# Opening two gate pairs with narrow products ahead of the plain feed-forward tiles

## The chip, the cores and the metric

The program runs on one core of a Trainium2 chip. The core has five engines that the text names as the profile does: PE (matrix products into the accumulation banks; PEld is its weight load), DVE (elementwise operations), ACT (activations and copies), POOL (here small scalars and DMA issues) and SP (DMA issues). Each engine works through its own list of instructions; semaphores make one wait for another. The metric is the device time of one launch in microseconds (us); less is better.

## What is computed

A two-layer decoder trunk on 512 tokens of width 1024 in float32: layer 0 has a gated short convolution, layer 1 windowed attention, and each layer ends in a SwiGLU feed-forward of inner width 2816. The change is in the feed-forward alone, which is run once per layer:

```python
def swiglu(h, w_gate_up, w_down):
    g, u = jnp.split(h @ w_gate_up, 2, axis=-1)
    return (jax.nn.silu(g) * u) @ w_down

for l in range(DEPTH):
    ...
    ff = swiglu(rmsnorm(h, ffn_pre_norm[l]), ffn_w_gate_up[l], ffn_w_down[l])
    h = h + rmsnorm(ff, ffn_post_norm[l])
```

## The kernel before

**Three products for one.** Every float32 factor is split into a high and a low part. `mm3` (L207) issues three matmuls for a product: high weight by low input, high by high, low weight by high input. A weight tile of 128x1024 arrives from memory as `raw`, ACT rounds it to `whi`, and DVE subtracts to get `wlo` (L500, L501).

**Plain tiles.** The inner width has 22 tiles of 128. The first two (`PLAIN = 2`) are plain: gate and up of each, so four products of 128 inner columns by all 512 tokens over eight blocks of the 1024 inputs. `project_first` (L1158) makes the four side by side in four banks (`pgu`). It goes over the first 256 tokens and then over the second 256, since those tokens' normalised input is finished later: after six blocks of the first half come the transposes of the last token tiles (`turn`), their splits (`split`), the copies of input parts (`keep`), and in the second half the seven-product factors (`factors`, L389). `gate_pair` (L1188) then applies Silu on ACT and the product with up on DVE.

**Gate pairs.** The other 20 tiles are ten pairs `q`. For each, gate and up of two tiles (256 columns) by the 512 tokens are a 2x2 block matrix, and `gate_jobs` (L1203) computes it in seven block products instead of eight. Product 1 is the gate's weights for the first half of the inputs by the first half of the tokens; product 2 the gate's weights for the second half of the inputs by the same tokens; 1 and 2 add up to the gate of the first 256 tokens. The other five (6, 5, 7, 3, 4) use sums of weight blocks and of input blocks (`factors`). A product has four blocks of inputs and two tiles `e`. The products run in the order 1, 2, 6, 5, 7, 3, 4. 1, 6, 7 and 4 are accumulated one upon the other in the two banks of chain X (tile `gx`), 5 and 3 in chain Z (`gz`), 2 has chain Y (`gy`). Chain X is *broad*: one matmul of 512 columns takes the high weight by high and low input side by side, and one of 256 the low weight by the high input. The others are narrow (`mm3` on 256 columns).

Because a chain goes on in the same bank, each stage has to be read out before the next product of the chain may write. `take(p)`, called right behind each product, does that: for 1, 6 and 4 ACT copies one half of each bank and DVE adds the other (L1260, L1237), for 7 DVE adds both halves, for 5 ACT copies, for 2 and 3 DVE adds. After 4, two DVE operations (L1264) multiply gate by up. `st`, `u` and `gr` are the tiles that hold these.

**The line of jobs.** `in_line` (L505) sets the order. Each product is a job; after job j it prepares the weights of job j+3 (ACT then DVE), then forms the sum of two raw tiles for the next one where a pair needs it (`add`, L488; pairs in `ADDED`, among them pair 1), then takes one part of the earlier pairs' input sums for the down product from a list (`pair_sums` L601: `a`, `s`, `alo`). Instructions of an engine stand in its list in this order. `manual_schedule` keeps it for PE, DVE, ACT and POOL; SP's DMA issues are placed by the scheduler. Behind pair 2 come the down products of the first round (`down_jobs`), then the next pairs.

**Weights in advance.** `Ahead` (L418) fetches and splits the first weights of a feed-forward while the stage before (`close`) still runs: four plain weights there, then two more that `last_tile` (L1132) splits between its steps; these are the blocks for products 1 and 2 of pair 0. There are 7 raw buffers and 4 pairs of weight buffers (`wsp`); `slots` puts a weight into other tiles instead. The pools of banks are `ps_mm` (4), `ps_sc` (2) and `ps_pt` (2).

Of the kernel before, what the change touches and what calls it, by code (L numbers as in the profile page):

```python
# [16 lines left out]
P = 128  # L17
D = 1024
S = 512
# [4 lines left out]

PLAIN = 2

ADDED = (1, 2, 3, 4, 5, 7)
# [56 lines left out]
def yoco_kernel(  # L84
# [46 lines left out]
    def wide(s, dt=F32):  # L131
        return wides.tile([P, D], dt, tag="wide", name=name(s))
# [124 lines left out]
    class Update:  # L257
# [130 lines left out]

        def factors(self):  # L389

# [7 lines left out]
            for j in range(2):  # L398
# [733 lines left out]
    def last_tile(res, pieces, ahead=None):  # L1132


        def some(i):
            for n, *f in pieces[i]:
                if n == "keep":
                    res.keep(f[0], 0, f[1])
# [18 lines left out]

    def project_first(pss, ws, x, then):  # L1158
        for hf in range(2):
            c = slice(hf * 256, (hf + 1) * 256)  # L1160

            for ks in ((0, 1), *((k,) for k in range(2, KT))):
                for ps, (whi, wlo) in zip(pss, ws):
                    for k in ks:
                        kk = slice(k * P, (k + 1) * P)
                        mm3(ps[:, c], whi[:, kk], wlo[:, kk],
                            x[k][0][:, c], x[k][1][:, c], k == 0, k == KT - 1)
                for k in ks:
                    then(hf, k)
# [12 lines left out]
    def ffn(l, before, ahead, gain, gpres, following):  # L1182
# [5 lines left out]
        def gate_pair(pg, pu):  # L1188
# [12 lines left out]
            return pair_sums(gr, acts[0])  # L1201

        def gate_jobs(q, factors, out, to, then):  # L1203


# [12 lines left out]
            pools = {"X": ps_mm, "Y": ps_pt, "V": ps_pt, "Z": ps_sc}  # L1218
            split = {}
            if q == 0:  # L1220

                pools = {"X": ps_sc, "Y": ps_pt, "V": ps_pt, "Z": ps_mm}
                raws[1], raws[2] = [], []
                split = {1: ahead.ready[4], 2: ahead.ready[5]}
            banks, kept = {}, []

            def tiles(a):
                return a.rearrange("p (e c) -> p e c", e=2)

            def take(p):  # L1230
                x, y, z, v = (banks.get(c) for c in "XYZV")
                st, u, gr = kept
                g0, g1 = (gr.rearrange("p (e h c) -> p e h c", e=2, h=2)[:, :, h]
# [4 lines left out]

                if p == 2:
                    add(g0, tiles(y), tiles(st))  # L1240
# [26 lines left out]
            def run(p):  # L1267
                def products(job):
                    if not kept:
                        kept.extend([slot("st"), slot("st"), wide("gr")])  # L1270
                    whi, wlo = split[p] if p in split else job.w
                    c = chain[p]
# [25 lines left out]
            def end():  # L1298
# [46 lines left out]
        mix = [None] * NB  # L1345
        pss = [bank("pgu", ps_mm) for _ in range(4)]
        with tc.manual_schedule(engines=ALL):
            last_tile(before, [
                [(0, 4)], [(0, 5), ("keep", 0, False), ("weights",)],
                [], [("keep", 1, True), (0, 6), (0, 7), ("keep", 3, True)],  # L1350
                [("keep", 2, False), ("weights",)]], ahead)

            def then(hf, k):
                if hf == 0 and k in (5, 6):
                    for b in ((0, 1), (2, 3))[k - 5]:
                        before.turn(b, (2,))
                if hf == 0 and k == 6:
                    for b in range(4):
                        before.turn(b, (3,))
                    for f in range(KT):  # L1360
                        before.split(0, f, 1)
                    for b in range(4):
                        before.keep(b, 1)
                if hf == 1 and k == 1:
                    factors.update(before.factors())
                if hf == 1 and k == 3:
                    if l == 0:
                        sum_on("o1")
                    sum_on(f"{l}f0")

            factors = {}
            project_first(pss, ahead.ready[:4], xs, then)

            def late():
                parts = [gate_pair(*pss[i : i + 2]) for i in (0, 2)][1]
                sum_on(f"{l}f1")
                return parts

            jobs, behind_one = [], []
            for rd, (f0, f1) in enumerate(ROUNDS):  # L1380
# [565 lines left out]
```

## Time and profile before

| what | value |
|---|---|
| median of 3 runs | 1010.04 us (1009.71 to 1010.2) |
| profiled execution | 1010.16 us |
| its span, first to last instruction | 1008.3 us |
| granted PE clock, mean | 0.998 |
| most frequent group on DVE: low parts of weights (L501) | x231, 279.0 us, mean 1212 ns |
| most frequent group on ACT: high parts of weights (L500) | x231, 239.7 us, mean 1051 ns |
| DMA moved | 246.61 MB, mean 245 GB/s |

The feed-forward of layer 0 begins near 176.7 us in the span, that of layer 1 near 671 us. Rows of the order of time give the start, the duration, the engine, the line, the operation, output and inputs, shapes and a count where equal ones follow each other; a bracket tells idle time ahead and who ended it. Successive instructions of DVE and ACT overlap by a little, so their price in a list is the distance from one start to the next.

### The profile page before, as it was taken

How to read it: one execution, taken by the hardware profiler on the slowest of the kernel's cores; microseconds unless marked ns; L12 is line 12 of the kernel's file. 1: busy time of each engine (PE TensorE's matmuls, PEld its weight loads, DVE VectorE, ACT ScalarE, POOL GpSimd, SP SyncE). 2: the span in 40 equal slices, each digit the busy share in tenths (PEclk: the TensorE clock that was granted, in tenths of full speed). 3: DMA queues.
4: the chain of work that ended last, by engine and by line, in shares of the span. 5: the costliest groups of instructions: out<-in, count | busy, mean ns of one | idle time of the engine just before them, and what ended most of it. 6: DMA issues, size and time to landing. Idle time of an engine off the chain costs nothing. (4 is left out here: it accounts for less than half of the span.)

```text
span 1008.3 us, 16460 instructions
## 1 busy us (share of the span) xinstructions
PE 999.5 (99%) x6008; PEld 887.4 (88%) x6008; DVE 911.2 (90%) x1564; ACT 609.5 (60%) x1105; POOL 184.6 (18%) x250
## 2 busy tenths in 40 slices
PE   9999999999999999999999999999999999999997
PEld 8899888999889898898898888799998988989986
DVE  7898877899799999999888998989997999999996
ACT  7445545875655455566485788777666564646641
POOL 0211021212101011000022756321201010110001
PEclk9999999999999999999999999999999999999999
DMA  9885988669979699779504889966999587978742
GB/s 342 266 253 172 335 291 289 200 198 286 342 236 298 225 301 317 241 217 333 198 1 136 216 241 250 278 259 170 311 281 315 167 253 239 300 259 271 244 169 83
DMA packets 67872, 246.61 MB, mean 245 GB/s; under 512 B 8016, under 2 KB 8784, under 8 KB 56016
## 3 DMA queue, kind: packets, MB, share of 16 engines
q1 hardware_dynamic: 52624, 148.14, 39.5%
q0 software_dynamic: 14592, 96.48, 37.6%
q8 instruction: 47, 0.77, 0.3%
q10 hardware_dynamic: 576, 0.95, 0.3%
q14 instruction: 33, 0.27, 0.1%
HBM read 239.25 MB, written 102.76 MB: 339 GB/s over the span
## 5 line engine op out<-in xcount | busy, mean ns | idle before, releaser
L501 DVE TENSOR_TENSOR wlo<-raw,whi 128x1024 fp32r<-128x1024 f32 (+1 forms) x231 | 279.0, 1212 | 26.5 <-ACT whi L500 26.3
L500 ACT ACTIVATE whi<-raw 128x1024 fp32r<-128x1024 f32 (+1 forms) x231 | 239.7, 1051 | 79.1 <-DVE raw L488 37.6
L1282 PE MATMUL gx<-xt,whi 128*128 128x512 f32 x480 | 120.6, 393 | 0.0
L1282 PEld LDWEIGHTS gx<-xt,whi 128*128 128x128 f32 x480 | 86.2, 189 | 15.7
L571 POOL DMA_DIRECT2D hsum<-in_w_gb_dram x96 | 63.7, 727 | 160.8 <-ACT whi L500 107.5
L571 POOL DMA_DIRECT2D hsum<-hsum x32 | 25.3, 790 | 351.5 <-ACT whi L500 257.7
L1260 ACT ACTIVATE st<-gx 128x256 f32<-128x256 f32 x120 | 43.5, 380 | 60.8 <-PE gx L1285 57.2
L1237 DVE TENSOR_TENSOR st<-gx,st 128x256 f32<-128x256 f32 x200 | 77.4, 417 | 2.2 <-ACT st L1260 0.4
L1285 PEld LDWEIGHTS gx<-xt,wlo 128*128 128x128 f32 x480 | 65.5, 190 | 4.7
L1285 PE MATMUL gx<-xt,wlo 128*128 128x256 f32 x480 | 66.9, 282 | 0.0
L1296 ACT ACTIVATE gr<-gr 128x1024 f32<-128x1024 f32 x20 | 21.2, 1062 | 55.8 <-DVE gr L1237 55.8
L208 PE MATMUL gy<-xlo,whi 128*128 128x256 f32 x176 | 49.8, 283 | 0.0
L209 PE MATMUL gy<-xhi,whi 128*128 128x256 f32 x176 | 49.8, 283 | 0.0
L210 PE MATMUL gy<-xhi,wlo 128*128 128x256 f32 x176 | 49.8, 283 | 0.0
L208 PE MATMUL px<-wlo,ahi 128*128 128x512 f32 x120 | 46.7, 389 | 0.0
L209 PE MATMUL px<-whi,ahi 128*128 128x512 f32 x120 | 46.7, 389 | 0.0
L210 PE MATMUL px<-whi,alo 128*128 128x512 f32 x120 | 46.7, 389 | 0.0
L571 POOL DMA_DIRECT2D hsum<-in_w_dn_dram x48 | 32.1, 765 | 69.0 <-ACT whi L500 47.4
L1282 PE MATMUL gx<-xhl,whi 128*128 128x512 f32 x160 | 39.9, 391 | 0.0
L672 DVE TENSOR_TENSOR mix<-mix,px 128x512 f32<-128x512 f32 x54 | 34.8, 679 | 2.1 <-PE px L210 2.1
L318 POOL TENSOR_TENSOR ur<-uv,mhalf 128x1 f32<-128x1 f32 x15 | 13.9, 928 | 115.0 <-DVE uv L313 114.9
L488 DVE TENSOR_TENSOR raw<-raw,raw 128x1024 f32<-128x1024 f32 x28 | 34.1, 1218 | 0.1
(359 smaller groups left out, 3052.4 us busy)
## 6 DMA issues: line engine op xcount, KB each, us to landing
hsum<-in_w_gb_dram POOLq DMA_DIRECT2D x96, 512.0 KB, 8.0
raw<-hsum SPq DMA_DIRECT2D x88, 512.0 KB, 8.1
raw<-in_w_gb_dram SPq DMA_DIRECT2D x60, 512.0 KB, 7.1
hsum<-in_w_dn_dram POOLq DMA_DIRECT2D x36, 512.0 KB, 8.0
raw<-in_w_dn_dram SPq DMA_DIRECT2D x32, 512.0 KB, 7.0
hsum<-hsum POOLq DMA_DIRECT2D x28, 512.0 KB, 5.6
hsum<-in_w_dn_dram POOLq DMA_DIRECT2D x12, 768.0 KB, 13.0
raw<-in_w_in_dram SPq DMA_DIRECT2D x13, 512.0 KB, 7.2
```

The source lines that it names most:

```text
L208: nc.tensor.matmul(out, whi, xlo, start=start, stop=False, **kw)
L209: nc.tensor.matmul(out, whi, xhi, start=False, stop=False, **kw)
L210: nc.tensor.matmul(out, wlo, xhi, start=False, stop=stop, **kw)
L488: nc.vector.tensor_tensor(out=raw, in0=raw, in1=self.raws[1].tile, op=ALU.add)
L500: self.begun = nc.scalar.activation(hi[:, :n], raw, AF.Copy)
L501: nc.vector.tensor_tensor(out=lo[:, :n], in0=raw, in1=hi[:, :n].bitcast(F32), op=ALU.subtract)
L571: nc.gpsimd.dma_start(dst, src, max_dma_last_dim=4 * 4 * S, **kw))
L672: nc.vector.tensor_tensor(out=m, in0=m, in1=banks[bs][r], op=ALU.subtract if half else ALU.add)
L1237: nc.vector.tensor_tensor(out=out, in0=a, in1=b, op=ALU.add)
L1260: nc.scalar.activation(ste, a, AF.Copy)
L1282: nc.tensor.matmul(banks[c][e], whi[:, kk], factors[p][k][2], start=opened and k == 0, stop=False, **kw)
L1285: nc.tensor.matmul(banks[c][e][:, :256], wlo[:, kk], factors[p][k][0], start=False, stop=k == 3 and p in (4, 5), **kw)
```

## The change

Two gate pairs (`OPENED = 2`) now begin ahead of the plain tiles. For each, products 1 and 2 are made narrow in one bank (`Opening`): product 1 over input blocks 0 to 3, a copy of the bank by ACT (`one`, into `st`), product 2 accumulated on top over blocks 4 to 7, and a copy of the sum by ACT into the gate's place (`two`, into `gr`). The four weights that are ready first are therefore those of these products; the four plain weights come behind. The plain tiles are then made one after the other over all 512 tokens (`project`), as four jobs at the head of the line. Pairs 0 and 1 have five jobs left, 6, 5, 7, 3, 4. Since their X chain begins at 6, product 1 has to be added by DVE: `take` for these pairs uses no ACT any more (four adds for 6 and 4, one for 5). Pair 1's first two blocks are still loaded in the line as well, for the sums that 6 and 3 need.

```diff
-        def factors(self):
+        def factors(self, between):
...
+                if j == 0:
+                    between()
...
     def first_weights(l):
-        return ([w_gu[l, f, j] for f in range(2) for j in range(2)]
-                + [w_gb[l, 0, b] for b in range(2)])
+        return ([w_gb[l, q, b] for b in range(2) for q in range(OPENED)]
+                + [w_gu[l, f, j] for f in range(PLAIN) for j in range(2)])
...
+        class Opening:
+            def __init__(self, q):
+                self.ws = ahead.ready[q], ahead.ready[OPENED + q]
+                self.x = bank("gx", ps_mm)
+                self.st, self.gr = slot("st"), wide("gr")
+
+            def products(self, *ks):
+                for k in ks:
+                    whi, wlo = self.ws[k // 4]
+                    for e in range(2):
+                        kk = slice(e * S + k % 4 * P, e * S + (k % 4 + 1) * P)
+                        mm3(self.x[:, e * 256 : (e + 1) * 256], whi[:, kk], wlo[:, kk],
+                            *(a[:, :256] for a in xs[k]), e == k == 0, e == 1 and k == KT - 1,
+                            skip_group_check=True)
+
+            def one(self):
+                nc.scalar.activation(self.st, self.x, AF.Copy)
+
+            def two(self):
+                out = self.gr.rearrange("p (e h c) -> p e h c", e=2, h=2)[:, :, 0]
+                nc.scalar.activation(out, self.x.rearrange("p (e c) -> p e c", e=2), AF.Copy)
...
+                if early and p == 6:
+                    both = slot("st")
+                    kept.append(both)
+                    for e in range(2):
+                        c = slice(e * 256, (e + 1) * 256)
+                        add(both[:, c], x[e][:, :256], st[:, c])
+                        add(both[:, c], x[e][:, 256:], both[:, c])
+                elif early and p == 5:
+                    add(u, z, st)
+                elif early and p == 3:
+                    add(g1, tiles(z), tiles(kept[3]))
+                elif early and p == 4:
+                    for e in range(2):
+                        c = slice(e * 256, (e + 1) * 256)
+                        add(st[:, c], x[e][:, :256], st[:, c])
+                        add(st[:, c], x[e][:, 256:], st[:, c])
...
-                    for p in (1, 2, 6, 5, 7, 3, 4)]
+                    for p in (1, 2, 6, 5, 7, 3, 4)[2 if early else 0 :]]
...
+            ahead.fetch(2)
+            opened_pairs = first, second = [Opening(q) for q in range(OPENED)]
+            for pair_of in opened_pairs:
+                pair_of.products(*range(4))
             last_tile(before, [
-                [(0, 4)], [(0, 5), ("keep", 0, False), ("weights",)],
-                [], [("keep", 1, True), (0, 6), (0, 7), ("keep", 3, True)],
+                [(0, 4)],
+                [(0, 5), ("keep", 0, False), ("do", first.one)],
+                [("do", second.one)],
+                [("keep", 1, True), (0, 6), (0, 7), ("keep", 3, True)],
                 [("keep", 2, False), ("weights",)]], ahead)
...
+            first.products(4, 5)
+            second.products(4, 5)
+            for b in range(2):
+                before.turn(b, (2,))
+            first.products(6, 7)
...
+            second.products(6, 7)
+            for f in range(KT):
+                before.split(0, f, 1)
+            first.two()
+            ahead.slots()
+            second.two()
+            ahead.hi()
+            for b in range(4):
+                before.keep(b, 1)
+            ahead.lo()
+            ahead.hi()
+            factors = before.factors(ahead.lo)
...
+            def plain_job(n):
+                def run(job):
+                    pss.append(bank("pgu", ps_mm))
+                    project(pss[n], ahead.ready[2 * OPENED + n], xs)
...
-            jobs, behind_one = [], []
+            jobs, behind_one = [plain_job(n) for n in range(2 * PLAIN)], []
```

What this does to the lists of the engines is shown at three places of layer 0. The first is DVE ahead of and at the taking of pair 1's product 6 (`gx` of pair 1 into `st`), which has to be over before PE may write product 7 on the same banks. Before:

```order
L614 TENSOR_TENSOR a_472_2476<-gr_2253,a_472_2476 128x256
L1237 TENSOR_TENSOR gr_2479<-gy_2510,st_2477 128x2x256
L501 TENSOR_TENSOR wlo_2537<-raw_2280,whi_2536 128x1024
L488 TENSOR_TENSOR raw_2233<-raw_2233,raw_2231 128x1024
L617 TENSOR_TENSOR s_2474<-gr_2253 128x256
L618 SCALAR_TENSOR_TENSOR s_2474<-s_2474,gr_2253 128x256
L1237 TENSOR_TENSOR st_2477<-gx_2480,st_2477 128x256
L1237 TENSOR_TENSOR st_2477<-gx_2481,st_2477 128x256
```

And now, where `gx_2288` and `gx_2289` are pair 0's banks and `gx_2450`, `gx_2451` pair 1's:

```order
L1250 TENSOR_TENSOR gr_1887<-gz_2320,st_2306 128x2x256
L505 TENSOR_TENSOR wlo_2407<-raw_2149,whi_2406 128x1024
L628 TENSOR_TENSOR alo_2411<-s_2284,ahi_2410 128x512
L1250 TENSOR_TENSOR st_1886<-gx_2288,st_1886 128x256 x2
L1250 TENSOR_TENSOR st_1886<-gx_2289,st_1886 128x256 x2
L1293 SCALAR_TENSOR_TENSOR gr_1887<-st_1886,gr_1887 128x2x256
L1293 SCALAR_TENSOR_TENSOR gr_1887<-st_2287,gr_1887 128x2x256
L505 TENSOR_TENSOR wlo_2438<-raw_2211,whi_2437 128x1024
L492 TENSOR_TENSOR raw_2247<-raw_2247,raw_2147 128x1024
L628 TENSOR_TENSOR alo_2443<-s_2285,ahi_2442 128x512
L1250 TENSOR_TENSOR st_2468<-gx_2450,st_1889 128x256
L1250 TENSOR_TENSOR st_2468<-gx_2450,st_2468 128x256
```

The end of pair 0 now stands two products ahead of this taking instead of four, and each bank has two adds on DVE instead of one on DVE and one copy on ACT.

The second place is PE where the plain tiles use the first input blocks (`xhl`) of the second 256 tokens. Before, narrow, with the next tile's bank after two blocks:

```order
L209 MATMUL pgu_1879<-xhl_1864,whi_1683 128x256
L210 MATMUL pgu_1879<-xhl_1864,wlo_1684 128x256
L208 MATMUL pgu_1880<-xhl_1861,whi_1689 128x256
L209 MATMUL pgu_1880<-xhl_1861,whi_1689 128x256
L210 MATMUL pgu_1880<-xhl_1861,wlo_1690 128x256
```

And now, behind the last matmuls of the second opened pair (`gx_1888`), whole:

```order
L211 MATMUL gx_1888<-xhi_1971,whi_1710 128x256
L212 MATMUL gx_1888<-xhi_1971,wlo_1711 128x256
L210 MATMUL pgu_2151<-xhl_1861,whi_1983 128x512
L211 MATMUL pgu_2151<-xhl_1861,whi_1983 128x512
L212 MATMUL pgu_2151<-xhl_1861,wlo_1985 128x512
L210 MATMUL pgu_2151<-xhl_1864,whi_1983 128x512
```

The narrow matmuls at the head now belong to the opened pairs, and a plain tile takes all tokens at once.

The third place is ACT in the last steps of the stage before (`last_tile`). Before:

```order
L387 ACTIVATE part_1904<-xt_1835,gt 128x256
L192 ACTIVATE whi_1906<-raw_1708 128x512
L192 ACTIVATE whi_1907<-raw_1708 128x512
L331 ACTIVATE junk_1615,us_519<-h_1264 128x1024
L369 ACTIVATE xhi_1919<-xt_1845,gt 128x256
```

And now:

```order
L389 ACTIVATE part_1958<-xt_1835,gt 128x256
L1212 ACTIVATE st_1886<-gx_1885 128x512
L333 ACTIVATE junk_1615,us_519<-h_1264 128x1024
L1212 ACTIVATE st_1889<-gx_1888 128x512
L371 ACTIVATE xhi_1967<-xt_1845,gt 128x256
```

The two halves of a weight have gone from here, and the copies of the two first products stand on both sides of the square of `h`; PE's second products wait for them.

More of the change, by code (lines that the diff above doesn't have):

```diff
@@ L25 @@
 PLAIN = 2
+OPENED = 2
 ADDED = (1, 2, 3, 4, 5, 7)
@@ L1136, in some @@
             for n, *f in pieces[i]:
-                if n == "keep":
+                if n == "do":
+                    f[0]()
+                elif n == "keep":
                     res.keep(f[0], 0, f[1])
@@ L1156, in last_tile @@
         some(4)
[L1158 to L1169, printed above, removed]
     def first_weights(l):
-        return ([w_gu[l, f, j] for f in range(2) for j in range(2)]
-                + [w_gb[l, 0, b] for b in range(2)])
+        return ([w_gb[l, q, b] for b in range(2) for q in range(OPENED)]
+                + [w_gu[l, f, j] for f in range(PLAIN) for j in range(2)])
     sum_on("o0")
@@ L1218, in gate_jobs @@
             pools = {"X": ps_mm, "Y": ps_pt, "V": ps_pt, "Z": ps_sc}
-            split = {}
             if q == 0:
                 pools = {"X": ps_sc, "Y": ps_pt, "V": ps_pt, "Z": ps_mm}
-                raws[1], raws[2] = [], []
-                split = {1: ahead.ready[4], 2: ahead.ready[5]}
             banks, kept = {}, []
+            early = opened_pairs[q] if q < OPENED else None
             def tiles(a):
@@ L1231, in take @@
                 x, y, z, v = (banks.get(c) for c in "XYZV")
-                st, u, gr = kept
+                st, u, gr = kept[:3]
                 g0, g1 = (gr.rearrange("p (e h c) -> p e h c", e=2, h=2)[:, :, h]
@@ L1237, in add @@
                     nc.vector.tensor_tensor(out=out, in0=a, in1=b, op=ALU.add)
-                if p == 2:
+                if early and p == 6:
[14 more added lines that the diff above has]
+                        add(st[:, c], x[e][:, 256:], st[:, c])
+                elif p == 2:
                     add(g0, tiles(y), tiles(st))
@@ L1269, in products @@
                     if not kept:
-                        kept.extend([slot("st"), slot("st"), wide("gr")])
-                    whi, wlo = split[p] if p in split else job.w
+                        kept.extend([early.st, slot("st"), early.gr] if early
+                                    else [slot("st"), slot("st"), wide("gr")])
+                    whi, wlo = job.w
                     c = chain[p]
@@ L1345, in ffn @@
         mix = [None] * NB
-        pss = [bank("pgu", ps_mm) for _ in range(4)]
         with tc.manual_schedule(engines=ALL):
+            ahead.fetch(2)
+            opened_pairs = first, second = [Opening(q) for q in range(OPENED)]
+            for pair_of in opened_pairs:
+                pair_of.products(*range(4))
             last_tile(before, [
-                [(0, 4)], [(0, 5), ("keep", 0, False), ("weights",)],
-                [], [("keep", 1, True), (0, 6), (0, 7), ("keep", 3, True)],
+                [(0, 4)],
+                [(0, 5), ("keep", 0, False), ("do", first.one)],
+                [("do", second.one)],
+                [("keep", 1, True), (0, 6), (0, 7), ("keep", 3, True)],
@@ L1351, in ffn @@
                 [("keep", 2, False), ("weights",)]], ahead)
[L1353 to L1369, printed above, removed]
@@ L1371, in ffn @@
-            factors = {}
-            project_first(pss, ahead.ready[:4], xs, then)
+            first.products(4, 5)
[3 more added lines that the diff above has]
+            first.products(6, 7)
+            for b in range(2, 4):
+                before.turn(b, (2,))
+            for b in range(4):
+                before.turn(b, (3,))
+            second.products(6, 7)
+            for f in range(KT):
+                before.split(0, f, 1)
@@ new lines, in ffn, with then @@
+            first.two()
+            ahead.slots()
+            second.two()
+            ahead.hi()
+            for b in range(4):
+                before.keep(b, 1)
+            ahead.lo()
+            ahead.hi()
+            factors = before.factors(ahead.lo)
+            pss = []
+            def plain_job(n):
+                def run(job):
+                    pss.append(bank("pgu", ps_mm))
+                    project(pss[n], ahead.ready[2 * OPENED + n], xs)
+                def then():
+                    if n == 0:
+                        if l == 0:
+                            sum_on("o1")
+                        sum_on(f"{l}f0")
+                    if n == 1:
+                        sum_on(f"{l}f1")
+                    return gate_pair(*pss[n - 1 :]) if n % 2 else None
+                return Job([], run, then)
@@ L1374, in late @@
             def late():
-                parts = [gate_pair(*pss[i : i + 2]) for i in (0, 2)][1]
-                sum_on(f"{l}f1")
-                return parts
-            jobs, behind_one = [], []
+                return []
+            jobs, behind_one = [plain_job(n) for n in range(2 * PLAIN)], []
             for rd, (f0, f1) in enumerate(ROUNDS):
```

## The prediction

> **What bounds the kernel now.** The page's span and first table come first, then the order of time on PE, then that on DVE.
>
> ```profile
> span 1008.3 us, 16460 instructions
> PE 999.5 (99%) x6008; PEld 887.4 (88%) x6008; DVE 911.2 (90%) x1564; ACT 609.5 (60%) x1105; POOL 184.6 (18%) x250
> ```
>
> PE's busy time includes modelled ends, so 99% alone proves little. The starts do: in these rows (start, duration, engine, line, tiles, count) matmuls follow each other at one pitch.
>
> ```profile
> 169.72 0.39 PE L209 MATMUL pmix<-whi,yhi 128*128 128x512 f32 x1
> ...
> 173.34 0.39 PE L210 MATMUL pmix<-whi,ylo 128*128 128x512 f32 x1
> 176.70 0.28 PE L208 MATMUL pgu<-xhl,whi 128*128 128x256 f32 x1
> ...
> 189.95 0.28 PE L208 MATMUL pgu<-xhl,whi 128*128 128x256 f32 x1
> 201.47 2.00 PE L1282 MATMUL gx<-xhl,whi 128*128 128x512 f32 x8
> ...
> 204.26 0.28 PE L208 MATMUL gy<-xlo,whi 128*128 128x256 f32 x1
> 207.14 2.00 PE L1282 MATMUL gx<-xt,whi 128*128 128x512 f32 x8
> 212.82 2.00 PE L1282 MATMUL gx<-xt,whi 128*128 128x512 f32 x8
> 221.28 2.00 PE L1282 MATMUL gx<-xhl,whi 128*128 128x512 f32 x8
> 226.96 2.00 PE L1282 MATMUL gx<-xt,whi 128*128 128x512 f32 x8
> 252.44 2.10 PE L1282 MATMUL gx<-xt,whi 128*128 128x512 f32 x8
> ```
>
> From 169.72 to 173.34 lie 16 steps of 512 columns: 0.226 us each. From 204.26 to 207.14 lie the 24 matmuls of one narrow product: 2.88 us, 0.120 each. A broad product (8 of 512, 8 of 256) takes 204.26-201.47 = 2.79. So PE has no time to give. Whatever makes it wait is added to the end, and whatever shortens its list is taken off.
>
> DVE is the engine next to it. In the stretches of gate pair 1 of both layers it is full:
>
> ```profile
> 223.10:243.00 19.90, 19.90 (x138) 18.52 (x137) 19.76 (x32) 12.45 (x20) 4.46 (x7) 1.00 0.78 236
> 717.40:737.30 19.90, 19.90 (x138) 18.52 (x137) 19.76 (x32) 12.46 (x20) 3.67 (x6) 1.00 0.98 335
> ```
>
> ```profile
> 263.00:300.00 37.00, 37.00 (x185) 31.42 (x184) 28.80 (x38) 21.47 (x30) 5.14 (x8) 1.00 0.83 266
> ```
>
> The columns are the stretch, its length, then busy time of PE, weight loads, DVE, ACT and POOL: DVE 19.76 of 19.90 us, and the same in layer 1, so that each term below counts twice. In the down products behind pair 2 (263 to 300) it is busy for 28.80 of 37. And once PE does touch it: its group at 252.44 (product 7 of pair 2) lasts 2.10 where the others last 2.00. It writes on the banks that DVE's two adds at 251.96 (below) read; the first of these ends near 251.96+0.42 = 252.38. From there to PE's start are 0.06 us. Seven products of PE work (19.84 us, by 4x2.79+3x2.88) are just enough to hide one pair's DVE work.
>
> **PE's own list.** Before, the four plain tiles took 201.47-176.70 = 24.77 us, 1 and 2 of pair 0 took 207.14-201.47 = 5.67, of pair 1 226.96-221.28 = 5.68: 36.12. After, the opening has 96 narrow matmuls and 16 transposes, as many as stood between 176.70 and 189.95: 13.25. The plain tiles then are 96 matmuls of 512: 96x0.226 = 21.7. That is 34.98, so **1.14 us less per layer**.
>
> The rows put a fixed part of 13 ns on each matmul (2x0.120-0.226). [...]
>
> **DVE's list.** These rows give the price of each kind, as steps from one start to the next:
>
> ```profile
> 208.05 0.42 DVE L614 TENSOR_TENSOR a<-gr,a 128x256 fp32r<-128x256 f32 x1
> 208.38 0.68 DVE L1237 TENSOR_TENSOR gr<-gy,st 128x512 f32<-128x512 f32 x1
> ...
> 210.12 0.41 DVE L617 TENSOR_TENSOR s<-gr 128x256 f32<-128x256 f32 x1
> 210.57 0.42 DVE L618 SCALAR_TENSOR_TENSOR s<-s,gr 128x256 f32<-128x256 f32 x1
> 210.91 0.75 DVE L1237 TENSOR_TENSOR st<-gx,st 128x256 f32<-128x256 f32 x2
> ...
> 216.34 1.67 DVE L1237 TENSOR_TENSOR st<-gx,st 128x256 f32<-128x256 f32 x4
> 217.93 1.21 DVE L501 TENSOR_TENSOR wlo<-raw,whi 128x1024 fp32r<-128x1024 f32 x1
> 219.06 0.68 DVE L624 TENSOR_TENSOR alo<-s,ahi 128x512 fp32r<-128x512 f32 x1
> 219.66 0.68 DVE L1237 TENSOR_TENSOR gr<-gz,st 128x512 f32<-128x512 f32 x1
> 220.26 1.22 DVE L501 TENSOR_TENSOR wlo<-raw,whi 128x1024 fp32r<-128x1024 f32 x1
> 221.40 1.22 DVE L488 TENSOR_TENSOR raw<-raw,raw 128x1024 f32<-128x1024 f32 x1
> ...
> 223.13 0.74 DVE L1237 TENSOR_TENSOR st<-gx,st 128x256 f32<-128x256 f32 x2
> 223.91 1.29 DVE L1264 SCALAR_TENSOR_TENSOR gr<-st,gr 128x512 f32<-128x512 f32 x2
> 225.12 1.22 DVE L501 TENSOR_TENSOR wlo<-raw,whi 128x1024 fp32r<-128x1024 f32 x1
> ...
> 251.96 0.75 DVE L1237 TENSOR_TENSOR st<-gx,st 128x256 f32<-128x256 f32 x2
> ```
>
> A weight's low part costs 1.13, a sum of two raw tiles 1.13, an operation on 512 columns 0.60, the first of the pair sums (a) 0.33, a pair of s 0.79, four adds 1.59. The two final multiplications cost 1.21, with 0.11 ahead of them. The new taking of product 4 (four adds, two multiplications) is thus 1.59+0.11+1.21 = 2.91. The new takings of 6 and 5 have the forms of the x4 row and of the 512 row; no other price is needed.
>
> The first place is product 7 of pair 1. PE accumulates it onto bank X after DVE has read product 6 from it, as the order rows show. Before, ACT took half of that reading. DVE can begin the taking of pair 0's product 6 no sooner than PE ends it, plus some 0.2 us, as ACT's copy after the narrow product that ended at 212.82:
>
> ```profile
> 213.02 0.60 ACT L1243 ACTIVATE st<-gz 128x512 f32<-128x512 f32 x1 [1.55 <-PE gz L210]
> ```
>
> From there, ahead of PE's release, DVE's queue holds: five low parts 5.65, two raw sums 2.26, four adds twice (6 and 7) 3.18, taking 5 and 3 1.20, two pairs of s 1.58, a 0.33, two alo 1.20, taking 4 2.91, and half of pair 1's four adds 0.86. Together 19.17. PE in that time has five products of pair 0 and 1 after 6, and pair 1's 5: 5, 7, 3, 4, 6, 5, that is 3x2.79+3x2.88 = 17.01. The **first wait** is 0.2+19.17+0.06-17.0 = 2.4 us.
>
> The second place is product 6 of pair 2, which needs its product 1 taken. From the first release DVE has: the other half of the adds 0.73, five low parts 5.65, two alo 1.20, taking 5 and 3 1.20, a 0.33, four adds 1.59, two pairs of s 1.58, a raw sum 1.13, taking 4 2.91, one add 0.41: 16.73. PE has 7, 3, 4, 1, 2: 3x2.79+2x2.88 = 14.13. The **second wait** is 2.6 us; some 0.3 of it falls already on pair 1's product 3, which needs 5 taken. A last one, product 7 of pair 2: rest of the adds 0.26, two low parts 2.26, two alo 1.20, taking 2 0.60, a raw sum 1.13, one add 0.41 = 5.86 against 2.79+2.88: 0.2. Behind pair 2 come the down products, where DVE has 8 of 37 us free (above) and works its lag off as now.
>
> Sum per layer: 2.4+2.6+0.2-1.14 = +4.0. Two layers: +8.0 on the profiled execution's 1010.16 (span 1008.3 and 1.9 around it; the median of the runs is 1010.04): **1018.2 us**.
>
> **What I cost at nothing.** The copies of the first products stand on ACT in place of a weight's two halves:
>
> ```profile
> 181.44 1.15 ACT L192 ACTIVATE whi<-raw 128x512 fp32r<-128x512 f32 x2
> 182.49 1.05 ACT L331 ACTIVATE junk<-h 128x1024 f32<-128x1024 f32 x1
> 183.43 0.19 ACT L331 ACTIVATION_READ_ACCUMULATOR junk<-h 128x1 f32 x1
> ```
>
> The first copy starts where the halves did and takes 0.60, the square and its read 1.04 or so, the second copy 0.60: it ends near 183.7, and PE wants that bank at 176.70+60x0.120 = 183.9. That is hidden by 0.2; without the cover it is up to 0.5 us per layer. The strided copy of the sum of 1 and 2 is not in the trace: the row at 213.02 (0.60) from below, twice that from above; I take 0.60, and the plain tile that reuses its bank comes over 10 us later, which hides both. The last plain weight's low part now stands behind half of the factors:
>
> ```profile
> 192.22 0.69 DVE L401 TENSOR_TENSOR part<-part,part 128x512 f32<-128x512 f32 x1 [0.42 <-ACT part L387]
> ...
> 203.01 1.22 DVE L501 TENSOR_TENSOR wlo<-raw,whi 128x1024 fp32r<-128x1024 f32 x1
> ```
>
> The factors took 203.01-192.22 = 10.8. With two weights' low parts (1.2 and 1.13) ahead, half of the factors and its own 1.13 it ends near 192.2+2.3+5.4+1.1 = 201, some 3 later if ACT, which also has two more weights, holds the factors up; PE wants it at 189.95+3x5.4 = 206. SP issues two more loads of 512 KB per layer (pair 1's first blocks, loaded again for their sums), and the load for pair 0's product 3 now stands behind the four writes of h:
>
> ```profile
> raw<-in_w_gb_dram SPq DMA_DIRECT2D x60, 512.0 KB, 7.1
> ```
>
> At 7 us to landing it is there ten us ahead of its split. If a load is late after all, DVE's list shifts by it: 0 to 1 us per layer. POOL's list is unchanged.
>
> **The rivals.** *No wait* (faster, 0.06): PE's release at pair 1's product 7 decides. If DVE needed 16.7 us there instead of 19.17, 13% less, and as much less at the second place, only PE's list would count: 1010.16-2.3 = 1007.9. ACT's lighter list speaks for it; the steps without idle time on DVE speak against. *The first wait alone* (0.14): the down weights and sums come in such an order that DVE has caught up by pair 2: 1010.16+2x(2.4-1.14) = 1012.7. Against it: nothing between the places is light on DVE. *The clock* (0.05): four waits of over 2 us end PE's full clock. The page's row has it at full throughout, so no row here shows what a pause does:
>
> ```profile
> PEclk9999999999999999999999999999999999999999
> ```
>
> If each wait made the next product take twice its 2.8 us, it would be 1018.2+11 = 1029. [...] *That the change doesn't do what it says* is out: the order rows show it.
>
> **How the numbers follow.** Forecast 0.75, first wait alone 0.14, no wait 0.06, clock 0.05. A tenth off DVE's prices moves each wait by some 1 us only if all are off one way; I take 1 us per layer below, and above as much plus 0.5 for the opening and 1 for a load. That is 1016 to 1023; down to the first-wait-alone case it is 1012.5 to 1023, with 0.11 left out by cases. A measurement of this kernel tells 0.2% (2 us) from no change. Faster has the 0.06 of no wait; 0.04 is for the part of the second case in which the wait is under 2.1 us, so that the end lies within 2 us; slower has the remaining 0.90.
>
> **What would show it.** In the new profile PE should pause ahead of the broad group of pair 1's product 7 by 2 to 3 us, released by DVE's add out of gx, and again at pair 2's 6; DVE should have no idle time between the takings. The plain tiles should step at 0.226 us. If DVE shows idle time in pair 1, the sum of its list is wrong; if PE pauses in the opening, the copies are what I missed; if the pauses are there and the end isn't later, something else on PE shrank.

## The result, and the profile after

| what | before | after |
|---|---|---|
| median of the timed runs | 1009.94 us (1009.71 to 1010.2, 4 runs) | 1019.01 us (1017.54 to 1020.04, 4 runs) |
| profiled execution, its span | 1010.16 us, 1008.3 us | 1019.24 us, 1017.5 us |

After over before is 1.0089, 95% interval 1.0071 to 1.0106: the change costs 9 us. The first table of the page of after hardly tells it:

```profile
span 1017.5 us, 16125 instructions
PE 999.8 (98%) x5848; PEld 879.5 (86%) x5848; DVE 914.6 (90%) x1572; ACT 603.1 (59%) x1085; POOL 184.5 (18%) x250
```

PE has 160 instructions fewer, as foreseen, yet its busy time is not shorter. The view of the waits, for PE, says where the time is (columns: line that waited, who released it, total, times, longest). Before:

```profile
PE idle L748 <- DVE ones L152: 1.1, 1, 1.1
PE pt L1603 <- DVE plo L1620: 0.4, 1, 0.4
PE pmix L208 <- DVE o L1651: 0.4, 1, 0.4
```

After:

```profile
PE gx L1312 <- DVE st L1250: 6.9, 4, 2.2
PE px L210 <- DVE mix L676: 1.5, 1, 1.5
PE idle L752 <- DVE ones L154: 1.1, 1, 1.1
PE pt L1654 <- DVE plo L1671: 0.4, 1, 0.4
PE pmix L210 <- DVE o L1702: 0.4, 1, 0.4
```

The two rows that are new are nearly the whole story; another new one, not shown, has 0.2. The first stands four times, twice per layer: the broad products wait for DVE's additions out of their banks. The order of time on PE, after, shows the four places and the one of the second row:

```profile
233.11 3.65 PE L1312 MATMUL gx<-xt,whi 128*128 128x512 f32 x8 [2.17 <-DVE st L1250]
...
240.43 2.00 PE L1312 MATMUL gx<-xt,whi 128*128 128x512 f32 x8
...
249.71 2.11 PE L1312 MATMUL gx<-xt,whi 128*128 128x512 f32 x8 [0.66 <-DVE st L1250]
...
290.30 0.50 PE L210 MATMUL px<-wlo,ahi 128*128 128x512 f32 x1 [1.47 <-DVE mix L676]
...
733.14 2.08 PE L1312 MATMUL gx<-xt,whi 128*128 128x512 f32 x8 [2.17 <-DVE st L1250]
...
749.74 2.11 PE L1312 MATMUL gx<-xt,whi 128*128 128x512 f32 x8 [1.90 <-DVE st L1250]
```

A bracket counts from the modelled end of the matmul before; by starts (step less the usual 0.12 or 0.23) each pause is 0.16 longer, and that is how pauses are given below: 2.33, 0.82 and 1.63 in layer 0, 2.33 and 2.06 in layer 1, where 0.25 more lie ahead of product 3 of pair 1. The group at 233.11 takes 3.65 instead of 2.00. The view by windows gives its granted clock (the third number from the right: 0.52):

```profile
233.10:236.30 3.20, 3.19 (x8) 2.55 (x9) 3.17 (x6) 2.36 (x4) 2.88 (x4) 0.52 0.92 238
```

The account, in spans: PE's list is 1.08 shorter in each layer (below), so 1008.3 - 2.16 + (2.33 + 1.65 + 0.82 + 1.63) + (2.33 + 0.25 + 2.06) = 1017.2; the profile has 1017.5. Two things that are not in this sum nearly cancel: the first steps behind the pauses are slower, which with the touches at product 7 of pair 2 makes some 0.7 in all, and the feed-forward of layer 0 begins 0.74 earlier in the span (175.96 against 176.70).

Why PE waits is in DVE's order of time, after, ahead of the first pause:

```profile
228.01 1.29 DVE L1293 SCALAR_TENSOR_TENSOR gr<-st,gr 128x512 f32<-128x512 f32 x2
229.22 1.22 DVE L505 TENSOR_TENSOR wlo<-raw,whi 128x1024 fp32r<-128x1024 f32 x1
230.35 1.22 DVE L492 TENSOR_TENSOR raw<-raw,raw 128x1024 f32<-128x1024 f32 x1
231.49 0.68 DVE L628 TENSOR_TENSOR alo<-s,ahi 128x512 fp32r<-128x512 f32 x1
232.09 1.66 DVE L1250 TENSOR_TENSOR st<-gx,st 128x256 f32<-128x256 f32 x4
```

Each instruction starts 0.08 to 0.09 before the one ahead of it has ended, so there is no gap. PE had ended its work by 230.8; the four additions that free its banks stand in the list behind two multiplications, a low part, a raw sum and an `alo`, and begin at 232.09. PE goes on at 233.11, when two of them are done.

### The profile page after: what moved, and what is told of

It reads as the page before. It is cut to its first block, busy times and chain, and to the rows that moved or that the text cites. A ratio compares the mean times of both kernels' runs of the same rounds, so it can differ in the third digit from the quotient of the medians.

```text
span 1017.5 us, 16125 instructions
## 1 busy us (share of the span) xinstructions
PE 999.8 (98%) x5848; PEld 879.5 (86%) x5848; DVE 914.6 (90%) x1572; ACT 603.1 (59%) x1085; POOL 184.5 (18%) x250
## 5 line engine op out<-in xcount | busy, mean ns | idle before, releaser
L505 DVE TENSOR_TENSOR wlo<-raw,whi 128x1024 fp32r<-128x1024 f32 (+1 forms) x227 | 274.2, 1213 | 26.1 <-ACT whi L504 26.0
L504 ACT ACTIVATE whi<-raw 128x1024 fp32r<-128x1024 f32 (+1 forms) x227 | 234.8, 1050 | 103.8 <-DVE raw L492 59.1
L1250 DVE TENSOR_TENSOR st<-gx,st 128x256 f32<-128x256 f32 x208 | 81.2, 418 | 4.7 <-PE gx L1315 2.0
L1289 ACT ACTIVATE st<-gx 128x256 f32<-128x256 f32 x96 | 34.7, 380 | 50.6 <-PE gx L1315 41.6
L210 PE MATMUL gy<-xlo,whi 128*128 128x256 f32 x144 | 40.8, 283 | 0.0
L211 PE MATMUL gy<-xhi,whi 128*128 128x256 f32 x144 | 40.8, 283 | 0.0
L212 PE MATMUL gy<-xhi,wlo 128*128 128x256 f32 x144 | 40.7, 283 | 0.0
L442 ACT ACTIVATE whi<-raw 128x1024 fp32r<-128x1024 f32 x18 | 19.3, 1082 | 23.6 <-DMA raw<-in_w_gb_dram 7.9
```

The costliest lines, as they stand in the source:

```text
L210: nc.tensor.matmul(out, whi, xlo, start=start, stop=False, **kw)
L211: nc.tensor.matmul(out, whi, xhi, start=False, stop=False, **kw)
L212: nc.tensor.matmul(out, wlo, xhi, start=False, stop=stop, **kw)
L504: self.begun = nc.scalar.activation(hi[:, :n], raw, AF.Copy)
L505: nc.vector.tensor_tensor(out=lo[:, :n], in0=raw, in1=hi[:, :n].bitcast(F32), op=ALU.subtract)
L1250: nc.vector.tensor_tensor(out=out, in0=a, in1=b, op=ALU.add)
```

## The experiments

Two theories are set against each other. By the first, DVE's list is too long for five products of PE (and too long again behind it), so time taken off DVE there comes back. By the second, something else holds PE, and DVE is merely the last to report: the order of products, the added loads, the clock.

**Less DVE, alone.** `a1_no_add` leaves pair 1's two raw sums out:

```diff
-            return [Job(raws[p], run(p), {3: gate, 4: end}.get(p), len(raws[p]) > 1)
+            return [Job(raws[p], run(p), {3: gate, 4: end}.get(p), len(raws[p]) > 1 and q != 1)
```

> The changed kernel with the two DVE sums of raw weight tiles of pair 1 left out in each layer (products 6 and 3 of pair 1 then use a block instead of a sum, so that part of the result is not computed); all loads stay. Theory, DVE's list: 2.26 us go from the list ahead of pair 1's product 7, so its pause of 2.33 falls to about 0.2 us in both layers; the pause at pair 2's product 6 stays at about 2.1. Time 1019.0-4.2 = 1014.8, and up to 1 less if the half-clock stretch goes too. Rival, the extra loads or the opening cost the time: the pauses stay, 1019.

Measured: 1015.02 us (1.0050 of before, 1.0035 to 1.0065). The views of the waits and of the order of time on PE show that only two of the four waits on chain X are left:

```profile
PE gx L1312 <- DVE st L1250: 3.8, 2, 1.9
```

and the one of layer 0:

```profile
247.64 3.11 PE L1312 MATMUL gx<-xt,whi 128*128 128x512 f32 x8 [1.91 <-DVE st L1250]
```

The pause at product 7 of pair 1 is down to 0.06 in both layers, that at product 6 of pair 2 is 2.07. No load was taken away and no product moved; 2.26 us less DVE work per layer brought 4.0 us, close to what DVE's list says.

**More DVE, in the kernel before.** `b1_more_dve` computes the low part of one weight of pair 1 three times, `b3_one_more` (`again = 1`) twice:

```diff
-            nc.vector.tensor_tensor(out=lo[:, :n], in0=raw, in1=hi[:, :n].bitcast(F32),
-                                    op=ALU.subtract)
+            for _ in range(1 + self.again):
+                nc.vector.tensor_tensor(out=lo[:, :n], in0=raw, in1=hi[:, :n].bitcast(F32),
+                                        op=ALU.subtract)
...
+            if q == 1:
+                line[4].again = 2
```

> The kernel before with the low part of one weight of pair 1 (that of product 7) computed three times instead of once: 2.27 us of DVE work more ahead of the taking of product 6, nothing else changed. Theory, DVE has no slack there: PE pauses ahead of pair 1's product 7 by about 2.1 us in both layers, and 1009.9 becomes 1014.1. Rival, DVE's lag is absorbed: 1010.

> The kernel before, with the low part of pair 1's product-7 weight computed twice (b1_more_dve: three times, 2.26 us more DVE, pauses of 2.42 and 1017.2); same output. DVE's list theory: 1.13 us more makes a pause of about 1.3 us per layer (b1's 2.42 less 1.13). If matmuls at half rate follow only the longer pauses, 1010.0+2.6 = 1012.6; if a pause of 1.3 brings them as well (b1 had 1.2 to 1.6 us of them per pause), 1015 to 1016. The rival that DVE's list has slack at that place: 1010 to 1011.

Measured: 1017.22 us for two more (1.0069, 1.0054 to 1.0084), 1012.40 for one more (1.0027, 1.0017 to 1.0037). The groups at product 7 of pair 1, layer 0, by the order of time on PE, in `b1_more_dve`:

```profile
234.53 3.39 PE L1284 MATMUL gx<-xt,whi 128*128 128x512 f32 x8 [2.26 <-DVE st L1239]
```

and in `b3_one_more`:

```profile
233.41 2.11 PE L1284 MATMUL gx<-xt,whi 128*128 128x512 f32 x8 [1.00 <-DVE st L1239]
```

So the kernel before had no slack at that place: one more operation of 1.13 makes a pause of 1.16 in both layers, two make 2.42. The smaller dose cost what its pauses say (1009.83+2x1.16 = 1012.2). The larger cost 3 us more than foreseen, because its matmuls then ran slowly (3.39 in place of 2.00) in both layers. With the 256-column matmuls behind them, some of which are slow too, product 7 takes 4.46 in place of 2.79, and 2x(2.42+1.67) = 8.2; the span is 7.5 longer (1015.8 against 1008.3), its first feed-forward having begun 0.5 earlier.

**ACT reads half of the banks again.** `a4_act_halves` gives back one part of the change:

```diff
-                        add(both[:, c], x[e][:, :256], st[:, c])
+                        nc.scalar.activation(both[:, c], x[e][:, :256], AF.Copy)
                         add(both[:, c], x[e][:, 256:], both[:, c])
+                    add(both, both, st)
...
-                        add(st[:, c], x[e][:, :256], st[:, c])
-                        add(st[:, c], x[e][:, 256:], st[:, c])
+                        nc.scalar.activation(kept[3][:, c], x[e][:, :256], AF.Copy)
+                        add(kept[3][:, c], x[e][:, 256:], kept[3][:, c])
+                    add(st, kept[3], st)
```

> The kernel after, with ACT again reading half of the banks of products 6 and 4 in pairs 0 and 1 (ACT copies the one half, DVE adds the other to it and then the whole to the kept product); nothing is left out. Of DVE's list 0.2 us go at each of these takings (1.59 becomes two adds of 0.40 and one of 0.60), and the first bank comes free after one add instead of two (0.4 earlier). DVE's list theory: the first pause falls from 2.33 to about 1.5, the pauses of a layer by some 1.1 in all: 1019.0-2.2 = 1016.8, and 1014 to 1015.5 if the matmuls at half rate go as well. Rival, that it isn't DVE's list but the order of products (PE needs the bank too early whoever reads it): 1019 with a pause of 2.3.

Measured: 1017.13 us (1.0073, 1.0058 to 1.0088). Its pauses in layer 0, from the order of time on PE:

```profile
232.66 2.12 PE L1314 MATMUL gx<-xt,whi 128*128 128x512 f32 x8 [1.43 <-DVE st L1250]
236.15 0.35 PE L210 MATMUL gz<-xlo,whi 128*128 128x256 f32 x1 [0.42 <-DVE st L1250]
249.36 2.14 PE L1314 MATMUL gx<-xt,whi 128*128 128x512 f32 x8 [1.65 <-DVE st L1250]
```

1.59, 0.58 and 1.81; layer 1 has the same. The first pause is what the list gave (1.5). Where DVE is the bound, as here, an ACT copy that takes 0.2 us off it and frees a bank 0.4 sooner is worth having: the first pause went from 2.33 to 1.59.

**Sums made in DRAM.** Pairs outside `ADDED` get their sums of weight blocks from POOL's transfers. `a2_sums1` takes pair 1 out of it, `a3_sums12` pairs 1 and 2 (in both, the second loads of pair 1's first blocks go as well); `b2_sums12` does the latter to the kernel before:

```diff
-ADDED = (1, 2, 3, 4, 5, 7)
+ADDED = (3, 4, 5, 7)
```

> The changed kernel with pair 1's sums of weight blocks made by DMA like pair 0's, so its two DVE sums and the two extra loads are gone and the result is complete. Theory, DVE's list: as without the sums, the first pause falls from 2.33 to about 0.2 us, the second stays near 2.1, 1014.8 us. Rival, loads: the same or better where fewer loads help, down to 1013; rival, DMA sums crowd the queues: above 1016, with pauses that a DMA ends.

> The changed kernel with the sums of pairs 1 and 2 by DMA. Theory, DVE's list: 4.5 us less DVE work per layer ahead of the second place; pauses 0.2 at pair 1's product 7, 0.3 at its product 3, 1.1 at pair 2's product 6: 1.6 per layer instead of 4.6, so about 1019.0-6 = 1013, or 1012 without a half-clock stretch. Rival, that PE's new order itself pauses it: 1019. Rival, DMA: more than 1015.

> The kernel before, with the sums of pairs 1 and 2 made in DRAM by POOL's transfers (as in a3_sums12, but without the opening); nothing is left out. It takes about 4.5 us of DVE work off the two pairs of each layer, and PE waits for none of it before. If the extra transfers are what cost a3_sums12 its gain, this kernel is late too, by about what a3 had of waits outside the gate pairs (0.65+0.51, 1.80, 4.5 in the attention stretch, 2.13: some 6 to 9 us): 1016 to 1019, with pauses between 590 and 660 us. If they are harmless without the opening, it stays at 1010, and a3's loss belongs to the opening's own extra loads.

Measured: 1016.67 us (1.0067, 1.0050 to 1.0084), 1021.66 (1.0120, 1.0103 to 1.0138) and 1018.87 (1.0091, 1.0075 to 1.0107). The first two missed what DVE's list alone gives (1014.8 and 1013). `a2_sums1` has the same row for chain X as `a1_no_add` (3.8, 2, 1.9), so the first wait went as foreseen; new waits of 0.6 and 0.7 stand in the attention of layer 1 (`pt`). In `a3_sums12`, by its view of the waits, those on chain X did fall, but others came:

```profile
PE gx L1312 <- DVE st L1250: 3.5, 3, 2.0
PE pt L1654 <- DVE plo L1671: 2.4, 3, 1.5
PE px L210 <- DVE mix L676: 1.6, 1, 1.6
```

and the same view of the control, `b2_sums12`, which has no opening, has them too:

```profile
PE px L208 <- DVE mix L672: 2.1, 1, 2.1
PE pt L1603 <- DVE plo L1620: 1.8, 2, 1.4
```

The sums in DRAM cost the kernel before some 9 us by themselves. On top of them the opening costs 1021.66 - 1018.87 = 2.8 us instead of 9: what DVE is relieved of comes back, and the transfers take more than that away, in the down products and in the attention of layer 1. These medians come from runs that spread by 4 us, so 2.8 is rough.

**Sums on POOL's vector unit.** `a5_pool_sums` computes the sums of pairs 1 and 2 there:

```diff
-                nc.vector.tensor_tensor(out=raw, in0=raw, in1=self.raws[1].tile, op=ALU.add)
+                self.eng.tensor_tensor(out=raw, in0=raw, in1=self.raws[1].tile, op=ALU.add)
...
+            if q in (1, 2):
+                for job in line:
+                    job.eng = nc.gpsimd
```

> The kernel after, with the raw sums of pairs 1 and 2 (four of 128x1024 per layer) computed by POOL's vector unit in place of DVE; nothing is left out and no transfer is added. DVE's list theory: the first pause goes as in a1_no_add (1015.0), and of the second about half (2.07 less 1.13 for pair 2's sum ahead of it): 1011 to 1013. If the second pause stays: 1015. POOL's price for such a sum isn't in the trace (1.30 us for 128x512 by its rows, so some 2.6); if that is too late for ACT's split, PE waits for a weight in front of product 6 or 7 (released by ACT) and the time is 1015 to 1020.

Measured: 1032.79 us (1.0225, 1.0208 to 1.0242), worse than every case named. Its order of time has POOL's sums

```profile
215.65 2.68 POOL L493 TENSOR_TENSOR raw<-raw,raw 128x1024 f32<-128x1024 f32 x1
...
243.10 2.51 POOL L493 TENSOR_TENSOR raw<-raw,raw 128x1024 f32<-128x1024 f32 x1 [7.03 <-DVE wlo L506]
```

and beside them on DVE

```profile
216.52 2.90 DVE L506 TENSOR_TENSOR wlo<-raw,whi 128x1024 fp32r<-128x1024 f32 x1
...
242.93 0.42 DVE L622 TENSOR_TENSOR s<-gr 128x256 f32<-128x256 f32 x1
243.39 2.51 DVE L623 SCALAR_TENSOR_TENSOR s<-s,gr 128x256 f32<-128x256 f32 x1
```

A low part takes 2.90 instead of 1.22, an operation that takes 0.42 elsewhere 2.51. POOL's sums end at 218.33 and 245.61, these two at 219.42 and 245.90, so 1.09 and 0.29 later, each 0.13 less than its usual time: as if DVE had begun them only when POOL was done. What holds DVE there isn't shown. Of 1.13 us saved per sum, DVE thus gives back 1.8 (216.52 to 218.33) and 2.2 (243.39 to 245.61), and PE's waits on chain X are the longer for it (12.7 us in four, the longest 5.5, against 6.9 and 2.2 in after); the granted clock is 0.990 over the span, against 0.997 in after.

**PE's term by itself.** `a7_no_sums` is `a4_act_halves` without any raw sum in pairs 0, 1 and 2; `b4_no_sums` is the kernel before without them; `a8_no_loads` is `a7_no_sums` without the second loads of pair 1's blocks. Pair 0 has no raw sums, so four per layer are left out, 4.5 us of DVE's work, and not the six of 6.8 us that the expectations count:

```diff
-            return [Job(raws[p], run(p), {3: gate, 4: end}.get(p), len(raws[p]) > 1)
+            return [Job(raws[p], run(p), {3: gate, 4: end}.get(p), len(raws[p]) > 1 and q > 2)
```

```diff
+            if q == 1:
+                raws[6] = raws[3] = raws[5]
```

> a4_act_halves with the raw sums of pairs 0, 1 and 2 left out of DVE (six of 128x1024 per layer; the loads stay), so those products are made with one block instead of a sum: that part of the result isn't computed. It is to show PE's term by itself: with DVE lighter by 6.8 us per layer, the walk of the lists leaves at most 0.7 us of pauses per layer, and PE's list is 1.14 shorter. Theory: 1009.9-2.3 = 1007.6 with no pause, up to 1009.0 with 0.7 per layer; under b4_no_sums by 1 to 2.3. Rival (the opening saves PE nothing, its matmuls are only renamed): 1010 or more, at or above b4_no_sums.

> The control of a7_no_sums: the kernel before with the same six sums per layer left out of DVE (that part of the result isn't computed). PE has no pause there to lose, so theory: 1009.5 to 1010, the same as before within 0.05%. Rival, that DVE's sums cost the kernel before something already: 1008 or less, and a7's gain would be DVE's.

> a7_no_sums with pair 1's products 6 and 3 made with the block of product 5 as it stands, so that the two blocks that the opening had are not loaded a second time: as many loads as in the kernel before (that part of the result isn't computed, as in a7). a7 had a pause of 1.30 us in the down products of layer 0 (near 286 us of its profile), behind a load that arrived late, and its five runs spread from 1012.0 to 1015.9. If the second loads crowd the transfers, that pause goes and the median falls to 1009 to 1010.5. If it is the changed place of the sums in DRAM, or chance, the pause stays at 1 to 2 us and the median at 1012 to 1015.

Measured: 1015.17 us (1.0051, 1.0037 to 1.0065), 1009.98 (1.0004, 0.9995 to 1.0013) and 1011.95 (1.0027, 1.0018 to 1.0036). The control is as expected: the kernel before gains nothing from a lighter DVE. `a7_no_sums` is a miss by 6 to 8 us, and by its median alone it falls on the side of the rival, that the opening saves PE nothing. What speaks for PE's term is the trace. Its profiled execution is the fastest of its five (1012.04), and its view of the waits has:

```profile
PE px L210 <- DVE mix L676: 1.1, 1, 1.1
PE idle L752 <- DVE ones L154: 1.1, 1, 1.1
PE gx L1314 <- DVE st L1250: 1.0, 2, 0.5
```

From the opening's first matmul (176.65) to the first down product (260.83) it takes 84.18 us, before 176.70 to 261.00, 84.30: PE's gain of 1.1 is there, and nearly as much is lost again: pauses of 0.24 and 0.66, more than the 0.7 of the walk, and the slower first steps behind them. Most of what that execution loses (1.9 against the profile of before), 1.3, is one pause in the down products, and `a8_no_loads` still has it, by the order of time on PE:

```profile
286.78 0.50 PE L210 MATMUL px<-wlo,ahi 128*128 128x512 f32 x1 [1.50 <-DVE mix L676]
```

So the second loads don't make that pause, and the opening isn't needed for one there: `b4_no_sums` has 0.6 and `b2_sums12` 2.3 at the same matmul of layer 0. Without the second loads the median of `a8_no_loads` is 3.2 us below that of `a7_no_sums` all the same, and why isn't shown. What the slower runs of `a7_no_sums` lose isn't shown, since no profile fell on one of them; two of them had a mean granted clock of 0.996 instead of 0.999.

**The kernel after, again.** `r1_after_again` is unchanged.

> The kernel after, unchanged, for a second profile: its pause of 2.33 us in layer 0 was followed by eight matmuls at 0.43 us a step, the same pause in layer 1 by none. If that is a matter of where the pause falls against something that runs by itself, the pauses are again 2.3 and 0.8 to 2.1, but the slow steps come behind others of them or behind none, and the profiled time differs by 1.65 us for each; 1017.5 to 1020. If it belongs to the place in the program, layer 0 shows them again and layer 1 doesn't.

Measured: 1020.08 and 1021.44 us (1.0107, 1.0089 to 1.0126), a little above the range. By the order of time on PE the slow steps have changed places:

```profile
233.57 2.08 PE L1312 MATMUL gx<-xt,whi 128*128 128x512 f32 x8 [2.17 <-DVE st L1250]
...
250.17 2.14 PE L1312 MATMUL gx<-xt,whi 128*128 128x512 f32 x8 [1.90 <-DVE st L1250]
...
733.96 3.15 PE L1312 MATMUL gx<-xt,whi 128*128 128x512 f32 x8 [2.17 <-DVE st L1250]
...
750.56 2.12 PE L1312 MATMUL gx<-xt,whi 128*128 128x512 f32 x8 [0.69 <-DVE st L1250]
```

The pauses of 2.33 are where they were; the half clock came behind the one in layer 1 this time. And in the layer where it came, the second pause shrank from 2.06 to 0.85.

No version tried here beats the kernel before; the best of the kernel after that leave nothing out are `a2_sums1` and `a4_act_halves`.

## Why the prediction was right, point by point

**PE's list, -1.14 per layer.** Right. The order of time on PE, after, has the first matmul of the opening, of the plain tiles, and of the product behind them:

```profile
175.96 0.28 PE L210 MATMUL gx<-xhl,whi 128*128 128x256 f32 x1
...
189.21 0.40 PE L210 MATMUL pgu<-xhl,whi 128*128 128x512 f32 x1
...
211.00 0.39 PE L1312 MATMUL gx<-xt,whi 128*128 128x512 f32 x1
```

13.25 for the opening and 21.79 for the tiles (13.25 and 21.7 said); 35.04 against 36.12 before is 1.08 less, and layer 1 has the same 35.04 (675.99 to 711.03). The fixed part of 13 ns on each matmul, read off two rows (2x0.120-0.226), decided this term: 1.08 over the 80 matmuls fewer is 13.5 ns each.

**The first wait, 2.4.** Right: 2.33 in both layers, in both profiles of after, at product 7 of pair 1, released by the addition out of `gx`. `a1_no_add` shows the cause from one side, `b3_one_more` from the other: the kernel before was without slack there, as the touch of 0.06 us in it, at the same place of pair 2, had suggested. The working came true as well as the number. From the end of pair 0's product 6 (213.76, where PE starts the next) to the restart at 233.11 lie 19.35, against 0.2+19.17+0.06 = 19.43 in the sum; DVE's rows in between are those that were listed, with one idle time of 0.22. Two additions in the prediction are off by 0.03 and 0.04 (13.25+21.7 is 34.95, 4x2.79+3x2.88 is 19.80), and no term hangs on it.

**The second wait, 2.6 with 0.3 of it at product 3.** Right in place, 0.3 too long: 0.25 and 2.06 in layer 1. In layer 0 it reads 0.82, since PE had been slowed by 1.65 in between and came later; 0.82+1.65 = 2.47.

**A last wait of 0.2 at product 7 of pair 2.** Half of it: ahead of that group, at 255.58 in after, the pause is 0.09, and its first step takes 0.11 more, as in the kernel before.

**Costed at nothing.** The copies of the opening were hidden, as said: 13.25 us without a pause. The last plain weight was in time (the tiles step at 0.227). For late loads 0 to 1 us per layer were allowed, which was too little for layer 0: it has 1.63 (2.01 in the second profile), layer 1 none. The order of time on ACT, after, has the load that was late:

```profile
285.60 1.06 ACT L504 ACTIVATE whi<-raw 128x1024 fp32r<-128x1024 f32 x1 [4.18 <-DMA raw<-hsum]
```

ACT's high part comes late, so DVE's low parts, and the additions that free `px` stand behind them. The transfers are dense in that stretch: the view by windows gives the share of the DMA engines (last column but one), in after

```profile
262.00:275.00 13.00, 13.00 (x63) 10.90 (x62) 10.09 (x15) 9.44 (x13) 2.19 (x3) 1.00 1.03 356
275.00:290.00 15.00, 13.83 (x62) 11.11 (x60) 9.01 (x13) 7.75 (x12) 1.21 (x3) 1.00 1.01 337
```

and before

```profile
262.00:275.00 13.00, 13.00 (x59) 10.77 (x58) 8.76 (x10) 8.12 (x10) 3.40 (x5) 1.00 1.04 328
275.00:290.00 15.00, 15.00 (x68) 12.43 (x67) 12.33 (x18) 8.00 (x12) 0.00 (x0) 1.00 0.91 338
```

A full stretch alone doesn't make the pause: `a4_act_halves` has 1.04 and 1.02 there and no pause. Whether POOL's later issues of the sums, the second loads or the shifted PE makes the load late stays open: `a8_no_loads`, which has the pause without the second loads, rules out that they alone do, and `a1_no_add` and `a4_act_halves`, which have them, show no such pause in their profiles.

**The rivals.** No wait and the first wait alone are refuted by the rows above. *The clock* was half right. No run recorded ahead of the prediction shows what a pause does to the clock, so its chance of 0.05 was the author's estimate. The runs showed that of pauses from 2.06 to 2.42 us some brought half clock. That it cost the kernel after so little is luck of the place: behind the first wait DVE is still late, so a slower PE only waits less at the second, and 2.33+1.65+0.82 = 4.80 in the layer with the slow steps compares with 4.64 in the one without. The timed runs agree: the three that were not profiled had a mean granted clock of 0.994 or 0.995 instead of 0.997, and took 1017.54 to 1020.04 us, on both sides of the profiled 1019.24. `b1_more_dve`, which has no second wait, paid in full.

The sum was 8.0 and the profile shows 9.2: the waits came out at 4.64 and 4.80 instead of 5.2 per layer, and the late load in layer 0, allowed for in the range only, put 1.63 on top. The two errors cancel in part, so that the number comes closer than its terms: that is luck. The two waits and PE's list, which make the sign and most of the size, came out as worked.

## What to carry to other kernels

Work taken off the bounding engine was worth nothing here, because the engine beside it had as long a list and less time for it: 1.1 us of PE per layer went, and five products instead of seven had to hide one pair's DVE work. Before such a change, walk the second engine's list from one release to the next with the prices of the trace. A cover that is exactly full can be found cheaply by a dose: one more operation in the kernel before, and see whether its whole price appears as a pause (here 1.13 us of DVE made one of 1.16).

## What was not expected of the hardware

**Half clock after short pauses.** Pauses of 1.16 to 1.81 us (`b3_one_more`, `a4_act_halves`) were followed by full steps each time (eight of 512 columns in 2.11 to 2.14 us). Of those of 2.06 to 2.42 in after, its second profile, `a1_no_add` and `b1_more_dve`, some were followed by a stretch at 0.43 us a step, 233.11 to 236.58 in after, and others of the same length by none; in `a1_no_add` the eight behind one took 3.11 us, in after 3.65.

The traces also tell which pauses bring it. By the view by windows, cut finely, the granted clock of after is 0.50 from 233.20 to 236.61 and 1.00 on both sides. Its trace records this stretch as 3.413 us, the full clock ahead of it (from 4.50) as 228.69 and the full clock behind it (to 1014.85) as 778.24, 67 and 228 times as long; in before the full clock lasts 996.69, 292 times as long. Counted in such periods, the pause of layer 0 in after (2.17 by its bracket) lay whole within the one ahead of the half clock, and the equal one of layer 1 was cut into 0.57 and 1.60. The other runs are counted from estimates of where their half clock begins. In `r1_after_again` the clock of 0.53 from 734.50 to 737.50 puts that at 734.68: the 2.17 of layer 1 lay whole within the period ahead of it, and of the pauses of layer 0, counted back in the same periods, no part was over some 1.7. In `b1_more_dve` 0.57 from 234.50 to 238.00 puts it at 235.0, with the 2.26 whole ahead of it; in `a1_no_add` 0.61 from 247.60 to 252.00 leaves the 1.91 whole ahead of it. A wait of 2.1 in the down products of `b2_sums12` brought no half clock (1.00 from 275 to 320), and how the periods fell there isn't shown. So in these traces it is a matter of where a pause of 2.3 us falls whether it costs half clock.

**DVE beside POOL's sums.** Operations of DVE that ran beside a sum on POOL took 2.51 us in place of 0.42 and 2.90 in place of 1.22, and ended 0.29 and 1.09 behind it (`a5_pool_sums`).
